# Matmuls on a buffer of zeros in the wait for the first loads

## The chip, the cores and the metric

One core of a Trainium2 chip runs the whole program. The metric is device time in microseconds (us) of one execution. Runs of the kernel before took 1066.47, 1067.73 and 1069.09 us; the median is 1067.73.

## The reference

Two groups of 512 tokens of width 1024 go through the same two layers. What matters for the change is the beginning of a layer (`c` is one conditioning row for each group):

```python
mod = jax.nn.silu(c) @ w_ada + b_ada
shift, scale, gate = jnp.split(mod, 3, axis=-1)
h = rmsnorm(x, g_norm) * (1.0 + scale[:, None, :]) + shift[:, None, :]
proj = h @ w_in
```

The projection feeds eight heads of dilated attention and four heads of retention. Their outputs are gated, joined, multiplied by `w_out`, scaled by the gate and added to `x`. A final RMS norm follows the second layer. All of it is float32.

## The kernel before

The large products are made in float32 accuracy out of rounded parts: a weight tile is split into a high half (`wH`, on ScalarE) and the rest (`wL`, on VectorE), and so is the normalised input, transposed (`hT`, 16 pieces: 8 slices k of 128 columns for each group b). `main_half` (line 839) adds three 128x512 matmuls for each k into a bank of PSUM: wH with the high half of hT, wH with its rest, wL with the high half.

**The beginning.** Lines 505 to 516 load the constants, the conditioning rows, the norm gains and the bias. VectorE clears `siluT`; ScalarE and VectorE make silu of the rows; PE transposes it and the gains (lines 523 and 524); VectorE writes them to `siluT` and `gcols`. The first columns of w_ada are then loaded in five pieces (line 760: k = 0, k = 1, then pairs). `first_mod` (578) multiplies a piece with `siluT` in column strips of 32, copies it, transposes it and makes the columns `acol` and `scol`. `first_x` (695) loads one of four tiles of x for each group, sums its squares on ScalarE, takes the inverse root on VectorE with ten tiny operations (`norm`, 685), and scales the tile on ScalarE. `first_h` (705) needs all four tiles of a group; for each k it transposes four blocks into a bank. `first_affine` (718) copies the bank to `xT` on VectorE, applies `acol` and `scol` and splits the result into hT. `prepper` (787) splits the weights. The first four items of the work list, with five output tiles, are computed early for the first group, one piece of k after another (lines 1275 to 1287); their five tiles hold five of the eight banks.

**The order.** Each engine runs its instructions in the order in which the program emits them, and that order comes from a planner in the same file. Each operation is noted with a cost (`Engine.cost`, 401), and `Plan.free["PE"]` is PE's planned time. The work is in generators; each yields a function that tells from which planned time on it is due (with a slack for what another engine makes). `pump` (214) asks all of them:

```python
now = self.free["PE"]
e = next((e for e in self.tasks if e[1]() <= now), None)
if e is None:
    t = ready()
    if t <= now:
        return
    e = min(self.tasks, key=lambda e: e[1](), default=None)
```

So what is due at PE's planned time goes first, in the order of the list, and only where nothing is due and PE would wait does the task with the earliest due time follow. The pieces' loads are issued by `pump(lambda: 0.0)` (line 1250), which runs all that is due at that time. A matmul's planned cost is `c = 0.4219 * n` for n columns, and `c + 12.0` where its operand is not float32 and its output has 128 partitions (lines 406 to 415).

All loads go through one queue, SP's. In the first 50 us it issues, in this order: constants, rows, four tiles of x, w_ada of piece 0, the first weight tile, w_ada of piece 1, four weight tiles, the rest of w_ada, and x of the second group.

Of the kernel before, what the change touches and what calls it, by code (L numbers as in the profile page):

```python
# [14 lines left out]
BF16 = mybir.dt.bfloat16  # L15
# [4 lines left out]
P = 128  # L20
# [28 lines left out]
LAT = 200.0  # L49
SLACK = {"PE": 200.0, "ACT": 400.0, "DVE": 900.0, "DMA": 1500.0}  # L50
SAME = {"DVE": 127.0}
NMAIN = 5
NBACK = 3
RLAG = 2
# [71 lines left out]
class Plan:  # L126
# [77 lines left out]
    def seen(eng, e):  # L204
        if e is None:
            return 0.0
        return e[0] + (SAME.get(eng, 0.0) if e[1] == eng else 260.0 if eng == "PE" else 180.0)

# [225 lines left out]
def trunk_kernel(  # L434
# [9 lines left out]
    V, A, T, Q = (Engine(plan, n, e) for n, e in (("DVE", nc.vector), ("ACT", nc.scalar), ("PE", nc.tensor),  # L444
                                                  ("SP", nc.sync)))
# [9 lines left out]
    H = Heap(plan, cp, "half", NHALF)  # L455
    B = Banks(plan, pp.tile([P, 8, 512], F32, name="banks"))
    W_RAW, W_W, W_T = Share(H, NRAW, NRAW, True), Share(H, NW, NW, True), Share(H, NTURN, NSURE, True)
    B_IN, B_BG = Share(B, NMAIN), Share(B, NBACK)

# [46 lines left out]
    rows, grow, th = (H.take(1, n)[:, 0:P] for n in ("rows", "grow", "th"))  # L506
# [4 lines left out]
    def mod_bias(l):  # L511
        t = H.take(1, "b6")
        Q.dma_start(t[0:6, :], b_ada[l:l + 1, :].rearrange("o (c n) -> (o c) n", n=512))
        return t

    bias = mod_bias(0)

    V.memset(siluT, 0.0)
    n16 = NB * KT
    A.activation(th[0:n16, :], rows[0:n16, :], AF.Tanh, scale=0.5)  # L520
    V.scalar_tensor_tensor(th[0:n16, :], th[0:n16, :], 1.0, rows[0:n16, :], op0=ALU.add, op1=ALU.mult)
    bk = B.take()
# [3 lines left out]
        V.tensor_scalar(siluT[:, :, b], bk[:, b * KT:(b + 1) * KT], 0.5, None, op0=ALU.mult)  # L526
    V.tensor_copy(gcols.rearrange("p l k -> p (l k)"), bk[:, 32:32 + n16])
    B.free(bk)
    H.free(rows, grow, th)

    COLS, GATES = ((0, 1), (2, 3)), ((4, 5), (4, 5))

# [736 lines left out]
    for l in range(DEPTH):  # L1269
# [77 lines left out]
        for b in range(NB):  # L1347
            for t in range(TT):
# [8 lines left out]
                for c, (n0, n1) in enumerate(LAST if final else ((0, D),)):  # L1357
                    for n, k in enumerate(KORDER):
                        pump(lambda: plan.soon(*yT[(k, b)], *wo[k]) if (k, b) in yT and k in wo else INF)
                        y, w = ([x.bitcast(F32R) for x in z] for z in (yT[(k, b)], wo[k]))  # L1360
                        for hy, hw in ((0, 0), (0, 1), (1, 0)):
                            for m in range(n0, n1, 512):
# [3 lines left out]
                                         start=(n == 0 and hy == 0 and hw == 0), stop=(n == KT - 1 and hy == 1))  # L1366
# [42 lines left out]
```

## Time and profile before

| | us |
|---|---|
| median of three runs | 1067.73 |
| the profiled execution | 1071.55 |
| span of its trace | 1069.8 |
| PE busy | 1041.6 (97%) |
| VectorE busy | 776.4 (73%) |
| ScalarE busy | 467.0 (44%) |

The profile is that of one execution. Its own time includes 1.75 us outside the span of the trace. PE is TensorE's matmuls and PEld its weight loads, DVE is VectorE, ACT is ScalarE, SP is the engine that issues the loads, and a "q" after an engine is its instruction queue. Names as `hT` or `wa` are those of the program; a buffer of the kernel's heap is reused under several names, and the trace shows only one of them (`dt` at ScalarE's first square is its scratch). Nearly every instruction carries line 385, the helper that records it, so the names tell the work apart. A float32 matmul of the small kind counts as two instructions.

### The profile page before, as it was taken

How to read it: one execution, taken by the hardware profiler on the slowest of the kernel's cores; microseconds unless marked ns; L12 is line 12 of the kernel's file. 1: busy time of each engine (PE TensorE's matmuls, PEld its weight loads, DVE VectorE, ACT ScalarE, POOL GpSimd, SP SyncE). 2: the span in 40 equal slices, each digit the busy share in tenths (PEclk: the TensorE clock that was granted, in tenths of full speed). 3: DMA queues.
4: the chain of work that ended last, by engine and by line, in shares of the span. 5: the costliest groups of instructions: out<-in, count | busy, mean ns of one | idle time of the engine just before them, and what ended most of it. 6: DMA issues, size and time to landing. Idle time of an engine off the chain costs nothing.

```text
span 1069.8 us, 14718 instructions
## 1 busy us (share of the span) xinstructions
PE 1041.6 (97%) x5443; PEld 832.8 (78%) x5443; DVE 776.4 (73%) x1616; ACT 467.0 (44%) x807; POOL 0.2 (0%) x4
## 2 busy tenths in 40 slices
PE   4999999999999999999999999999999999999997
PEld 3678676877777787777888878878888787777886
DVE  5598665688956898786547776579857896777555
ACT  6365422425533266674234562326534364665011
POOL 0000000000000000000000000000000000000000
PEclk9899999999999999999999999999999999999998
DMA  9906998048992469975222698046961749692222
GB/s 313 367 5 207 232 268 278 21 148 244 261 301 111 159 168 280 245 186 204 79 88 70 215 189 263 23 137 181 236 157 58 236 106 256 167 261 99 95 103 79
DMA packets 217336, 189.64 MB, mean 177 GB/s; under 512 B 156656, under 2 KB 167184, under 8 KB 217264
## 3 DMA queue, kind: packets, MB, share of 16 engines
q1 hardware_dynamic: 217264, 188.69, 63.0%
q8 instruction: 43, 0.70, 0.3%
q14 instruction: 29, 0.24, 0.1%
HBM read 117.34 MB, written 33.57 MB: 141 GB/s over the span
## 4 chain that ended last, share of the span: by engine, by line
PE 83%; DMA 6%; DVE 5%; SPq 3%; ACT 2%; issue 2%; DVEq 0%; ACTq 0%
PE banks L385 83%; DMA wa<-in_w_ada_dram 3%; SPq L385 3%; DMA pT<-pt 1%; DMA stk_dram<-rc 1%; DVE nst L385 1%; DMA KL<-stk_dram 1%; ACT pt L385 1%; DVE sS L385 1%; ACT sS L385 1%; DVE dt L385 1%; DVE xT L385 0%; DVE hT L385 0%; DVE rsq L385 0%; DMA stk_dram<-b 0%
## 5 line engine op out<-in xcount | busy, mean ns | idle before, releaser
L385 PE MATMUL banks<-hT,wH 128*128 128x512 f32 x1536 | 478.7, 393 | 2.9 <-DVE hT L385 2.8
L385 PEld LDWEIGHTS banks<-hT,wH 128*128 128x128 f32 x1536 | 286.9, 188 | 72.4 <-issue 9.8
L385 PE MATMUL banks<-hT,wL 128*128 128x512 f32 x768 | 300.2, 391 | 0.0
L385 PE MATMUL banks<-wo,yT 128*128 128x512 f32 (+1 forms) x792 | 176.2, 384 | 0.0
L385 PEld LDWEIGHTS banks<-hT,wL 128*128 128x128 f32 x768 | 144.7, 188 | 30.2
L385 PEld LDWEIGHTS banks<-wo,yT 128*128 128x128 f32 x792 | 145.2, 188 | 29.3 <-issue 0.4
L385 PE MATMUL banks<-wH,hT 128*128 128x256 f32 x512 | 97.5, 285 | 0.0
L385 PEld LDWEIGHTS banks<-wH,hT 128*128 128x128 f32 x512 | 81.7, 192 | 6.3 <-issue 5.4
L385 DVE TENSOR_TENSOR wL<-raw,wH 128x1024 fp32r<-128x1024 f32 x56 | 67.9, 1220 | 13.3 <-ACT wH L385 13.2
L385 PE MATMUL banks<-wL,hT 128*128 128x256 f32 x256 | 72.5, 283 | 0.0
L385 ACT ACTIVATE sS<-sS,sm 128x512 f32<-128x512 f32 x88 | 62.6, 713 | 19.0 <-DVE sm L385 18.6
L385 ACT ACTIVATE wH<-raw 128x1024 fp32r<-128x1024 f32 x56 | 58.5, 1052 | 27.5 <-DMA raw<-in_w_in_dram 21.7
L385 DVE SCALAR_TENSOR_TENSOR pt<-sS,sm,pt 128x512 f16<-128x512 f32 x88 | 61.8, 746 | 3.7 <-ACT pt L385 3.6
L385 DVE CUSTOM_DVE_ANT_0 sS<-banks,tabs 128x512 f32<-128x512 f32 x88 | 57.1, 686 | 9.3 <-PE banks L385 9.3
L385 ACT ACTIVATE pt<-sS,sm 128x512 f16<-128x512 f32 x88 | 58.7, 710 | 11.7 <-DVE sm L385 7.2
L385 ACT ACTIVATE sq<-xr 128x1024 bf16<-128x1024 f32 (+2 forms) x15 | 14.2, 944 | 92.9 <-DVE xr L385 44.3
L385 DVE TENSOR_TENSOR res<-banks,gb 128x512 f32<-128x512 f32 (+1 forms) x33 | 22.2, 671 | 43.5 <-PE banks L385 43.5
L385 PEld LDWEIGHTS banks<-wL,hT 128*128 128x128 f32 x256 | 49.0, 192 | 0.8
L385 PE MATMUL banks<-sr,rv 128*128 128x512 f32 x167 | 47.0, 392 | 0.0
L385 PE MATMUL banks<-pT,vn 128*64 128x512 f16 x384 | 45.6, 381 | 0.9 <-DMA pT<-pt 0.8
L385 PE MATMUL banks<-wa,siluT 128*32 128x128 f32 (+1 forms) x384 | 34.5, 413 | 8.7 <-DVE nst L385 5.9
L385 PEld LDWEIGHTS <-vn 128*64 128x64 f16 x384 | 21.9, 110 | 21.7 <-issue 6.4
(314 smaller groups left out, 1270.5 us busy)
## 6 DMA issues: line engine op xcount, KB each, us to landing
raw<-in_w_in_dram SPq DMA_DIRECT2D x56, 512.0 KB, 5.1
wa<-in_w_ada_dram SPq DMA_DIRECT2D x48, 512.0 KB, 7.5
KL<-stk_dram SPq DMA_DIRECT2D x49, 256.0 KB, 5.2
KS<-stk_dram SPq DMA_DIRECT2D x48, 256.0 KB, 4.7
QS<-stk_dram SPq DMA_DIRECT2D x46, 256.0 KB, 3.4
rawo<-in_w_out_dram SPq DMA_DIRECT2D x16, 512.0 KB, 4.7
stk_dram<-rs SPq DMA_DIRECT2D x31, 256.0 KB, 6.4
stk_dram<-rc SPq DMA_DIRECT2D x30, 256.0 KB, 5.9
```

The lines of the kernel that those rows point to most:

```text
L385: r = fn(*args, **kw)
```

## The change

A half buffer of zeros is taken and cleared on VectorE, ahead of `siluT`, and one bank of PSUM is taken. Matmuls of 128x128 by 128x512 in bfloat16, with zeros for both operands, write this bank, each for itself: 9 ahead of the first two transposes, 24 behind them and ahead of everything else that PE does. Bank and buffer are then given back. Nobody reads the bank's contents. The zero matmuls go through the same recording helper as all others, so their cost enters the planner.

```diff
+WARM = (9, 24)
...
+    zero = H.take(1, "zero")
+    V.memset(zero.bitcast(BF16), 0.0)
     V.memset(siluT, 0.0)
     n16 = NB * KT
+    idle = B.take()
+
+    def keep_warm(n):
+        for _ in range(n):
+            T.matmul(idle, zero.bitcast(BF16)[:, 0:P], zero.bitcast(BF16)[:, 0:512], start=True, stop=True)
+
+    keep_warm(WARM[0])
     A.activation(th[0:n16, :], rows[0:n16, :], AF.Tanh, scale=0.5)
...
     V.tensor_copy(gcols.rearrange("p l k -> p (l k)"), bk[:, 32:32 + n16])
     B.free(bk)
-    H.free(rows, grow, th)
+    keep_warm(WARM[1])
+    B.free(idle)
+    H.free(rows, grow, th, zero)
```

## Rows read from the trace of the kernel before

**Rows 1.** The profile page, parts 1 (busy time) and 4 (chain)

```profile
PE 1041.6 (97%) x5443; PEld 832.8 (78%) x5443; DVE 776.4 (73%) x1616; ACT 467.0 (44%) x807; POOL 0.2 (0%) x4
...
PE 83%; DMA 6%; DVE 5%; SPq 3%; ACT 2%; issue 2%; DVEq 0%; ACTq 0%
```

**Rows 2.** Waits of PE from 48 us: total, times, longest

```profile
PE banks L385 <- DMA wa<-in_w_ada_dram: 1.7, 4, 0.8
...
PE banks L385 <- DVE hT L385: 0.2, 1, 0.2
```

**Rows 3.** Stretches of PE: length, busy (instructions), granted clock, DMA share, GB/s

```profile
5.40:12.25 6.85, 0.95 (x6) 1.00 1.08 367
...
28.00:30.55 2.55, 0.00 (x1) 0.83 1.10 349
...
34.20:36.50 2.30, 2.30 (x41) 0.50 1.10 348
```

**Rows 4.** Groups of 12:18, 18:21.1, 24.1:25.1 us: busy us, mean ns

```profile
L385 PE MATMUL banks<-wa,siluT 128*32 128x128 f32 x32 | 4.2, 420 | 7.0 <-DVE nst L385 5.9 <-DMA wa<-in_w_ada_dram 1.1
...
L385 PE MATMUL banks<-small,x 128*128 128x128 f32 x12 | 2.8, 426 | 0.0
...
L385 PE MATMUL banks<-small,x 128*128 128x128 f32 x8 | 1.1, 281 | 0.0
```

**Rows 5.** Chain of waits up to 31 us: start, us, what

```profile
5.13 8.79 DMA wa<-in_w_ada_dram
...
13.97 3.64 PE banks L385 x30
...
18.06 6.16 PE banks L385 x49
```

**Rows 6.** Two more stretches of PE

```profile
31.14:33.70 2.56, 2.56 (x7) 0.50 1.10 348
59.72:61.76 2.04, 2.04 (x10) 1.00 0.00 0
```

**Rows 7.** Timeline of ACT and DVE, x tiles: start, us, what

```profile
0.85 0.27 DVE L385 MEMSET siluT<- 128x256 f32 x1 [0.85 <-PEq L1394]
...
6.06 0.86 DVE L385 TENSOR_SCALAR selg<-small 128x128 fp32r<-128x128 f32 x4
...
7.68 0.53 DVE L385 TENSOR_SCALAR nst<-nst 128x1 f32<-128x1 f32 x3 [0.76 <-ACT dt L385]
...
13.61 0.52 DVE L385 TENSOR_SCALAR nst<-nst 128x1 f32<-128x1 f32 x3
...
15.51 0.16 DVE L385 TENSOR_TENSOR nst<-nst 128x1 f32<-128x1 f32 x1
15.76 1.15 ACT L385 ACTIVATE x<-x,nst 128x1024 f32<-128x1024 f32 x1 [0.82 <-DVE nst L385]
```

**Rows 8.** Timeline of SP, DVE and ACT, up to hT of k = 0

```profile
10.85 1.43 SPq L385 DMA_DIRECT2D wa<-in_w_ada_dram  x1
...
18.43 0.23 DVE L385 SCALAR_TENSOR_TENSOR acol<-banks,gcols 128x1 f32<-128x1 f32 x2 [0.52 <-PE banks L385]
...
18.64 1.22 DVE L385 TENSOR_TENSOR wL<-raw,wH 128x1024 fp32r<-128x1024 f32 x1
...
24.30 1.06 ACT L385 ACTIVATE wH<-raw 128x1024 fp32r<-128x1024 f32 x1 [0.55 <-DMA raw<-in_w_in_dram]
...
26.37 0.67 DVE L385 COPY xT<-banks 128x512 f32<-128x512 f32 x1
...
29.24 0.53 DVE L385 TENSOR_SCALAR dt<-dt,acol,scol 128x512 f32<-128x512 f32 x1
29.80 0.69 DVE L385 TENSOR_TENSOR hT<-dt,hT 128x512 fp32r<-128x512 f32 x1
```

**Rows 9.** Timeline of PE, and chain of waits, 76 to 79 us

```profile
76.62 0.95 PE L385 MATMUL banks<-hT,wH 128*128 128x512 f32 x2
...
78.26 29.46 PE banks L385 x127
```

## The prediction

> **What bounds the kernel now.** I read the page first [rows 1]: PE is busy 97% of the span and carries 83% of the chain that ended last. So the time is the moment at which PE begins to work without a break, plus PE's work, plus the few waits after that. The waits after 48 us sum to 1.7 + 0.8 + 0.7 + 0.7 + 0.2 = 4.1 us [rows 2]; nearly all of PE's idle time lies ahead of 30.55 us, which is the stretch that the change touches.
>
> Second, the stretch windows of PE [rows 3]. The reader is to see that PE is idle in 5.40 to 12.25 (0.95 of 6.85 us busy) and in 28.00 to 30.55, and that from 30.55 on it is full. The granted clock reads 1.00 up to 28 us, but the durations say otherwise [rows 4]: the small matmuls on wa average 420 ns in 12 to 18 us, the transposes 426 ns in 18 to 21.1 and 281 ns after 24.1. So PE ran at 1.2 GHz until it rose to 2.4 within 21.64 to 24.2, after it had been at work since 18.06. The column does not show it; I go by durations. A second low stretch is recorded: 0.83 in the idle 28.00 to 30.55, then 0.50 until about 36.5.
>
> Third, the chain of waits up to 30.55 [rows 5]: 8.79 us of DMA for the first w_ada tiles (landed 13.92), PE's 30 matmuls of piece 0 in 3.64 us, PE again 6.16 us, then DVE alone until hT of k = 0 is split at 30.50. The change can win on the PE links of this chain, 9.8 us, and on the low clock after it.
>
> **What is added.** One memset of 128x1024 bf16: the nearest row is the 128x256 f32 memset, 0.27 us [rows 7], so 0.27 to 1.08 us by size; DVE's next work is at 5.06, so it is hidden. 33 matmuls of 512 columns: no such bf16 one is in the trace. The nearest are the main matmuls of the same shape: in 59.72 to 61.76 nine start in 2.04 us at full clock (0.227 each), in 31.14 to 33.70 six in 2.56 at half (0.427; each count in [rows 6] has one more, which only ends there). From about 1.5 us on, nine at half are 3.85 us, to 5.4: the two first transposes (5.39) move by 0 to 0.4 us, which has cover until 12.28. The 24 are 5.4 us at full clock and 10.2 at half: they end between 11.3 and 16.1. I take 12, near the full end, since PE will then have been at work without a break, as it was ahead of the rise seen in rows 4. The w_ada tile lands at 13.92, so they are hidden; if they all ran at half, piece 0 is 2.1 us late.
>
> **What moves, and this is the larger part.** The emission order of every engine comes out of the planner, and the zeros advance its clock of PE. By its cost line a 512-column bf16 matmul is 0.4219 x 512 + 12 = 228 planned ns, so the 24 put PE's planned time 5.5 planned us later at the very point where `pump(lambda: 0.0)` asks which tasks are due. (These are planner units, used for the order alone.) Before, nothing but loads is due there. After, by following the due times by hand, x tile 0 is due for its whole normalisation and tiles 1 to 3 for their squares. ACT then issues: square 0, scaled copy 0, squares 1, 2, 3, copy 1, wH of the first weights, copies 2, 3. Before, copy 0 stood behind squares 0 to 2. Square 1 now waits for DVE's chain of tile 0 and copy 0. And the four selg scalings of DVE (0.86 us), which now fill a gap at 6.06, fall behind the chain of tile 0.
>
> In trace time [rows 7]: square 0 ends 7.65, DVE's chain 0 runs 7.68 to 9.75, copy 0 1.15 us to 10.93, square 1 with its read to 12.2, then DVE's chains 1 to 3 at 1.97 us each to 18.2. Before, chain 3 ended at 15.67. So DVE is 2.5 us late with x, and all transposes of x (they need all four tiles) wait until copy 3 ends at 19.35, against 18.32 before. Piece 0 now leaves PE about 15.8 instead of 17.6, but DVE takes it up only at 18.2. What the faster PE wins there, the x chain gives back.
>
> After that, by hand again, PE has piece 1 ahead of the transposes of x, and DVE has: copy of piece 0, wL, acol/scol, copy of piece 1, wL, acol/scol, xT, wL, xT, wL, scaling of xT, wL, split of hT. Piece 1's second tile was issued at 10.85; with the first one's 8.79 us it lands about 19.65 (no later than 21.64, where PE did not wait for it). Its 32 matmuls take 3.6 us at half (30 took 3.62) and 1.8 at full clock as half of that. DVE's copy of it ends 21.85 at full clock, 23.65 at half. Behind it stand 4 wL x 1.22 + 0.23 for acol + 2 x 0.67 + 0.53 + 0.69 = 7.67 us of DVE [rows 8], so hT of k = 0 is complete at 29.5 or 31.3, against 30.49: **-1.0 or +0.8**. I take -1.0, as PE is then in a nearly unbroken run and the floor by the last early weight (ACT 24.30 + 1.06, wL 1.22, 0.53, 0.69: 27.8) does not bind.
>
> One price more: only 3 banks stay spare beside the 5 early ones, and each holds a group of 4 transposes until DVE copies it. With DVE late, 5 of the 8 groups are done before the main matmuls and 12 transposes fall into the full stretch, where nothing hides them. Eight took 1.1 us at full clock, twelve 2.8 at half [rows 4]: **+1.65** (to +2.8; 0 if I misplace them).
>
> By the Trainium skill ("TensorE: Matmul & The Clock Gate", Part 4, on PE-mode transposes) the full clock does not engage for transposes, and the twelve would be priced at 2.8. The trace disagrees: 281 ns after 24.1 against 426 before.
>
> The second low stretch (30.55 to 36.5, 5.95 us, half lost: 3.0 us) I leave as it is: PE still idles before the split of hT, from about 26.4 to 29.6, and a shorter idle stretch ended in the fall before. Bounds: -3.0 to 0.
>
> From 48.31 to 78.26 the chain runs over ACT and DVE (x of the second group, decays, hT) [rows 9], and PE waits at its end 0.22 us, with 0.33 more inside the pair at 76.62 (0.95, against 0.62 for the pair before it). If PE comes later this takes **-0.55** back; if it comes earlier, DVE's chain keeps most of that gain unless its start moves too.
>
> **Sum**: -1.0 + 1.65 - 0.55 = +0.1 us. The profiled execution took 1071.55 (span 1069.8 and 1.75 around it), so 1071.65; the median of the runs shown, 1067.73, is 3.82 lower, so **1067.8**. What can be told from no change is 0.3%, 3.2 us; this is no change.
>
> **Rivals.**
> *PE stays fast.* The clock, once up, stays up through the first waits, the x chain costs less than I work out, and the second fall is gone too: hT at the floor, 27.8, is -2.7, the low stretch -3.0, together 1062.0. For it: PE's links on the chain are 9.8 us. Against it: the clock fell in the idle stretch of 2.55 us from 28.00 on [rows 3], and idle stretches of about 2 us (12 to 13.9) and 2.7 (15.8 to 18.5) remain.
> *The order falls luckily.* All later choices of the planner see a shifted PE time; at best the 4.1 us of later waits go: about 1063.8. Nothing but the 4.1 bounds it.
> *Warmth is lost in the gap* (the slower side). PE has nothing between 15.8 and 18.5, the clock falls there, piece 1 runs at half: hT +0.8, twelve transposes at half +2.8, and -0.55: +3.05, 1070.8; from a fall ahead of about 20 us on it decides. For it: the same fall.
> [...]
> *Zeros do not raise the clock.* The 24 end at 16.1, piece 0 at 19.7, piece 1 about 24.0, hT 31.95 (+1.5), +2.8, -0.55: +3.75, 1071.5.
>
> **Chances.** My forecast 0.42; PE stays fast 0.18; lucky order 0.14; warmth lost 0.18 (half of it over the 0.3%, as later waits add to it); zeros useless 0.08. The order of work after 60 us may shift either way by as much as the 4.1 us of waits. So faster 0.32, same 0.44, slower 0.24. Range for 8 in 10: from below the lucky cases, 1061, to above the useless zeros, 1072.5. The forecast's own range is 1065.5 to 1070.
>
> **What would show it.** ACT's order: copy 0 directly behind square 0, copy 3 after 18 us. Right: DVE's x chain ends near 18. Wrong: the old order, with copy 3 at 15.8. wa matmuls of pieces 0 and 1 far below 420 ns (420 for piece 1 would be the slower rival). The second main matmul at 29.6 (below 28.5: PE stays fast; above 31: slower). Twelve transposes of x after it. The granted clock at 0.50 again for 4 to 6 us behind it. PE's waits after 48 us near 4 us; a sum over 8 would make the prediction wrong from a place that I could not price.

## The result, and the profile after

| | before | after |
|---|---|---|
| median of four runs each, us | 1068.03 (1066.47 to 1069.09) | 1080.7 (1080.14 to 1082.15) |
| ratio, with its 95% interval | | 1.0105 (1.0083 to 1.0127) |
| the profiled execution, us | 1071.55 | 1082.15 |
| span of its trace, us | 1069.8 | 1080.3 |

The change makes the kernel 1.05% slower by the ratio, which is 11.2 us; the medians of the table lie 12.67 us apart. The forecast was no change, 1067.8, and the range ended at 1072.5. The cause of the main slower rival, lost warmth, did not decide the time. One execution of a later run (LAT 150 with zeros) took 5379.28 us and is left out of its ratio.

The page after, parts 1 (busy time) and 4 (chain), the answers to [rows 1]:

```profile
PE 1049.5 (97%) x5476; PEld 833.6 (77%) x5476; DVE 776.1 (72%) x1617; ACT 468.5 (43%) x808; POOL 0.2 (0%) x4
...
PE 83%; DMA 6%; DVE 4%; SPq 3%; ACT 1%; issue 1%; ACTq 0%; DVEq 0%
```

PE has 33 instructions and 7.9 us more of busy time, and its share of the chain is as before. The page alone does not say where 10.5 us of span came from: the 33 zero matmuls stand in a wait, and do not lengthen the span by their own time. The profiled execution of before is itself 3.5 us above its median, so these 10.5 us tell two executions apart and not the medians. I cut the trace at 48 us, where the beginning is over. These are the windows of PE (stretch, length, busy and count, granted clock, DMA share, GB/s), first of the kernel before, then after:

```profile
0.00:48.00 48.00, 32.06 (x356) 0.93 1.02 338
48.00:1069.80 1021.80, 1009.58 (x5088) 1.00 0.62 170
```

```profile
0.00:48.00 48.00, 38.55 (x397) 0.93 1.01 336
48.00:1080.30 1032.30, 1010.93 (x5081) 1.00 0.61 168
```

From 48 us on PE is busy 1.35 us longer (1010.93 against 1009.58) and idle 21.37 us instead of 12.22: **9.15 of the 10.5 us are new idle time behind the stretch that the change touches.** The waits of PE from 48 us on name it (total, times, longest), against the five rows and 4.1 us of [rows 2] (first a row of before that does not stand there):

```profile
PE banks L385 <- DMA pT<-pt: 0.8, 2, 0.5
```

```profile
PE banks L386 <- DMA wa<-in_w_ada_dram: 4.8, 4, 2.6
PE banks L386 <- DMA pT<-pt: 3.3, 4, 1.6
PE banks L386 <- DVE yT L386: 2.9, 2, 2.0
PE banks L386 <- DMA QS<-stk_dram: 1.1, 1, 1.1
PE banks L386 <- DMA KL<-stk_dram: 0.7, 2, 0.6
PE banks L386 <- ACT yT L386: 0.4, 1, 0.4
```

The six of the kernel after sum to 13.2 us. Three of them were not there before (yT twice, QS); those on w_ada and pT have grown by 3.1 and 2.5; before's waits on yr and hT are gone. The largest single wait, 2.6 us, ends at 122.78. SP's queue shows what it waits for (start, us, what), and PE's timeline the end of it:

```profile
103.79 14.34 SPq L386 DMA_TRANSPOSE pT<-pt  x4
118.22 1.01 SPq L386 DMA_DIRECT2D wa<-in_w_ada_dram  x2
...
122.78 2.92 PE L386 MATMUL banks<-wa,siluT 128*32 128x512 f32 x8 [2.55 <-DMA wa<-in_w_ada_dram]
```

PE's row for the next eight of this shape in the kernel before:

```profile
128.82 1.07 PE L385 MATMUL banks<-wa,siluT 128*32 128x512 f32 x8
```

Two tiles of w_ada are issued at 118.22, behind four transposes by DMA that hold SP's queue for 14.34 us, and PE's order has the eight matmuls on them at 120.2. Before, the pair of loads behind four transposes was issued 4.5 us later, at 122.75 (its row stands below), and the next eight matmuls of this shape began at 128.82, without a wait: PE now asks for them at 120.23, 8.6 us earlier, while SP sends them only 4.5 us earlier. This wait has a second price, in the windows of PE around it and of the beginning:

```profile
14.65:18.00 3.35, 3.31 (x30) 0.55 1.21 305
...
29.02:32.10 3.08, 3.08 (x7) 0.51 1.10 349
...
120.20:122.80 2.60, 0.05 (x3) 1.00 0.88 306
122.80:126.40 3.60, 3.45 (x10) 0.70 1.07 256
126.40:132.00 5.60, 5.60 (x24) 0.89 1.16 265
```

After the wait the granted clock is 0.70 for 3.60 us and 0.89 for 5.60: 0.30 x 3.60 + 0.11 x 5.60 = 1.7 us lost. That is more than the 1.35 us by which PE is busier from 48 us on, so by this count PE has 0.35 us less work left at 48 us than it had before: all that the zeros win in the beginning of this execution.

### The profile page after: what moved, and what is told of

Its sections match the earlier page's. It is cut to its first block, busy times and chain, and to the rows that moved or that the text cites. A ratio compares the mean times of both kernels' runs of the same rounds, so it can differ in the third digit from the quotient of the medians.

```text
span 1080.3 us, 14817 instructions
## 1 busy us (share of the span) xinstructions
PE 1049.5 (97%) x5476; PEld 833.6 (77%) x5476; DVE 776.1 (72%) x1617; ACT 468.5 (43%) x808; POOL 0.2 (0%) x4
## 4 chain that ended last, share of the span: by engine, by line
PE 83%; DMA 6%; DVE 4%; SPq 3%; ACT 1%; issue 1%; ACTq 0%; DVEq 0%
PE banks L386 83%; SPq L386 3%; DMA wa<-in_w_ada_dram 2%; DMA pT<-pt 1%; DMA KL<-stk_dram 1%; DVE hT L386 1%; DMA raw<-in_w_in_dram 1%; DVE pt L386 1%; DVE wL L386 1%; DMA KS<-stk_dram 1%; DVE sS L386 0%; DVE rc L386 0%; ACT pt L386 0%; DMA stk_dram<-rc 0%; DVE rsq L386 0%
## 5 line engine op out<-in xcount | busy, mean ns | idle before, releaser
L386 PEld LDWEIGHTS banks<-hT,wH 128*128 128x128 f32 x1536 | 287.0, 189 | 74.3 <-issue 13.2
L386 ACT ACTIVATE sS<-sS,sm 128x512 f32<-128x512 f32 x85 | 60.4, 712 | 21.1 <-DVE sm L386 20.6
L386 ACT ACTIVATE sq<-xr 128x1024 bf16<-128x1024 f32 (+2 forms) x18 | 17.3, 963 | 115.2 <-DVE xr L386 71.3
```

What stands on the lines that cost most here:

```text
L386: r = fn(*args, **kw)
```

## The experiments

Each ratio is against runs of the kernel before on the same chip. Two theories stood at first. **O**: the zeros cost nothing where they stand, but as they go through the planner they advance its time of PE, the whole order is drawn anew, and this draw is worse. **A**: the added work itself costs (PE's sequence, the clock, the bank, the buffer). The expectations call it rival Z; what they call A is the bank and the buffer alone.

**The zeros without the planner.** They are issued past the recording helper, so the planned order is that of before, instruction by instruction; in the traces, PE, DVE and ACT keep it, apart from the zeros and one memset.

```diff
+    zero = diff.bitcast(BF16)[:, 0:512]
+    nc.vector.memset(zero, 0.0)
...
+            nc.tensor.matmul(B.t[:, 7, :], zero[:, 0:P], zero, start=True, stop=True)
```

> The 33 zero matmuls stand where the change has them, but are issued without a note in the planner, out of a buffer and a bank that it does not count, so that every other instruction has the order of the kernel before. Theory O (the loss is the order that the planner draws once its PE clock is moved): no loss; PE runs piece 0 and the first transposes at full clock, hT of k = 0 is complete about 29.1 us instead of 30.49, and the time is 1064 to 1067 against 1068.0. Rival Z (the zero matmuls themselves cost PE or its clock later on): 1078 or more, as with the change.

**The planner without the zeros.** Each zero matmul is noted with its cost, none is issued.

```diff
-            T.matmul(idle, zero.bitcast(BF16)[:, 0:P], zero.bitcast(BF16)[:, 0:512], start=True, stop=True)
+            z = zero.bitcast(BF16)
+            plan.note("PE", T.cost("matmul", [idle], [z[:, 0:P], z[:, 0:512]]), [idle], [z[:, 0:P], z[:, 0:512]])
```

> The planner notes the 33 zero matmuls, with buffer and bank, but none of them is issued: the order of every engine is that of the change, without zeros on the chip (the zero buffer is still cleared). Theory O: as slow as the change, 1080 to 1084, since the low clock of the beginning comes back. Rival Z: 1066 to 1070, as the kernel before.

Measured: zeros alone 1073.08 against 1069.25, ratio **1.0024** (1.0005 to 1.0043); order alone 1077.71, ratio **1.0086** (1.0057 to 1.0116). Neither time lies in the range that O had given it, but by ratio both are nearer to O than to Z. What the planner makes of the zeros, with not one zero matmul issued, carries 0.86 of the 1.05%; that is the new order together with the buffer and the bank that the noted zeros take, which this run does not part. In the traces the order of PE (without the zeros), DVE, ACT and SP agrees with the kernel after, instruction by instruction. Part of the loss is low clock: the five executions have a mean granted clock of 0.9916, the 30 of before beside them 0.9969. That is an estimated 5.7 us of the 8.7 by which their mean times differ. Its two largest waits of PE from 48 us on are again of the kinds that the kernel after shows:

```profile
PE banks L386 <- DMA pT<-pt: 3.1, 2, 2.1
PE banks L386 <- DVE yT L386: 1.6, 2, 0.9
```

But the longest wait of the kernel after is missing. The loads behind the four transposes, and the eight matmuls on them:

```profile
116.62 1.13 SPq L386 DMA_DIRECT2D wa<-in_w_ada_dram  x2
...
121.37 1.81 PE L386 MATMUL banks<-wa,siluT 128*32 128x512 f32 x8
```

The transposes held SP's queue for 12.45 us here and for 14.34 with the zeros, in the same order. So the wait of 2.55 us is not the order's alone; this run loses its time elsewhere, most visibly at 472 to 490 us, where PE waits on yT four times and the granted clock reads 0.81.

The run of the zeros alone is the more instructive one, for it has the change as it was meant and still gains nothing. Its timeline of PE:

```profile
14.25 1.93 PE L386 MATMUL banks<-wa,siluT 128*32 128x128 f32 x30 [1.28 <-DMA wa<-in_w_ada_dram]
...
28.95 0.50 PE L386 MATMUL banks<-hT,wH 128*128 128x512 f32 x1 [1.37 <-DVE hT L386]
...
75.21 0.50 PE L386 MATMUL banks<-hT,wH 128*128 128x512 f32 x1 [0.22 <-DVE hT L386]
...
114.04 1.05 PE L386 MATMUL banks<-wa,siluT 128*32 128x512 f32 x4 [1.48 <-DMA wa<-in_w_ada_dram]
```

Piece 0 takes 1.93 us where it took 3.64 [rows 5], the second main matmul starts at 28.95 where it started at 30.55, and no later fall of the clock is recorded. At 75.21 it starts the very matmul that started at 78.26 before [rows 9]: 3.05 us ahead. Not all of this belongs to the zeros. The profiled execution of before had its clock fall from 28 us on [rows 3], and many have not: of 107 executions of before in these runs 52 have a mean granted clock of 0.998 or more, which leaves under 3 us of lost clock in the whole span, and the profiled one has 3.4 in its first 48 us (0.07 x 48). A run without zeros that has the same order of PE (w_ada on a second queue, below) starts this matmul at 76.15, 2.1 us ahead.

Then a new wait of 1.48 us on w_ada stands at 114.04. The two tiles were issued at 106.19 (107.59 before), and the second is there at 115.33 (115.60 before): issued 1.4 us earlier, it lands 0.3 us earlier, and that is all that is left of PE's lead. SP's queue behind them, before and then with the zeros alone:

```profile
108.52 14.18 SPq L385 DMA_TRANSPOSE pT<-pt  x4
122.75 1.24 SPq L385 DMA_DIRECT2D wa<-in_w_ada_dram  x2
```

```profile
107.20 16.39 SPq L386 DMA_TRANSPOSE pT<-pt  x4
123.64 1.05 SPq L386 DMA_DIRECT2D wa<-in_w_ada_dram  x2
```

The same four transposes are issued 1.3 us earlier, hold the queue 2.2 us longer, and the loads behind them go out 0.9 us later. In this execution starting earlier did not mean finishing earlier. It is no rule: the eight matmuls that begin at 128.82 before begin as follows with the zeros alone, with more zeros in the second gap, and in the change with PE's time put back (the last two are below):

```profile
128.55 1.81 PE L386 MATMUL banks<-wa,siluT 128*32 128x512 f32 x8
```

```profile
126.00 1.75 PE L386 MATMUL banks<-wa,siluT 128*32 128x512 f32 x8
```

```profile
125.19 1.90 PE L386 MATMUL banks<-wa,siluT 128*32 128x512 f32 x8
```

The lead is 0.3, 2.8 and 3.6 us. The second loses it at 178.40, in a wait of 2.75 us on w_ada; the third, the fastest of ten executions, keeps it as long as its order is that of before (the same matmul at 895.23 and 891.33). The first ends 2.5 us behind before, and loses most of that after 130 us. So the traces do not agree on where the lead goes.

**More warmth.** If the clock is the point, the next gap of PE (from 26.4 to hT) should be worth filling too. 20 more zero matmuls of 256 columns follow the first main matmul, again unseen by the planner.

```diff
+            if fill:
+                for _ in range(fill.pop()):
+                    nc.tensor.matmul(out[:, 0:256], zero2[:, 0:P], zero2, start=False, stop=False)
```

> As the run with unseen zeros, and 20 more unseen zero matmuls of 256 columns behind the first main matmul, added into its bank, where PE waits 2.56 us for the split of hT. Theory O with the low clock as a cost of its own: the clock does not fall near 30 us, the main matmuls from there on take 0.227 us each and not 0.427, and 1 to 3 us are won on top of the first run: 1061 to 1066. Rival Z: slower than the first run.

Measured: 1072.22, ratio 1.0019 (0.9999 to 1.0038), no better than without them. It was to reach 1061 to 1066. The trace of the zeros alone was already free of the second fall, so there was nothing for it to win there.

**Other draws of the order.** If the order is what counts, other numbers of planned zeros must give other times, whether zeros run or not. First the change with 34 for 24, then the change with PE's planned time put back behind the 24, then 8, 20 and 15 planned ones of which none is issued.

```diff
-WARM = (9, 24)
+WARM = (9, 34)
```

> The change with 34 zeros in the second group instead of 24; the planner sees them and draws a third order. The ten more end before the first w_ada tile lands (14.6 us), so on the chip they cost nothing. Theory O: the time is that of another draw and differs from the change's 1080.7 by more than 3 us, to either side (the planner's own end is 5 planned us earlier than for the change). Rival Z: 1080 to 1083.

```diff
+    now = plan.free["PE"]
     keep_warm(WARM[1])
+    plan.free["PE"] = now
```

> The change as it is, 33 zeros through the planner with buffer and bank, but PE's planned time is put back behind the 24 to what it was ahead of them. The planner then draws the order of the kernel before (its planned times agree up to PE's matmul 4414 of 5211). Theory O, by the planned clock: 1.000 to 1.005 of the kernel before, as with unseen zeros (1.0024). Rival A (the buffer half and the bank that the zeros take shift all later buffers): 1.008 or more, as with the change.

```diff
-WARM = (9, 24)
+WARM = (9, 8)
```

> Only the planner sees zeros, none is issued, and 8 in the second group instead of 24: enough that the square of x's first tile is due early, too few for the rest. Theory O: another draw, with a time of its own between 0.998 and 1.012 of the kernel before, not the 1.0086 of the 24. If a moved planned clock were bad by itself, the loss would go with its size: 1.003.

> Only the planner sees zeros, 20 in the second group. Its own end is 1.3 planned us ahead of the kernel before, where that of the 24 is 2.5 behind. Theory O with a planner that knows its work: 0.997 to 1.001 of the kernel before. If the planner does not know what a draw costs on the chip (as for the 34, which it put 2.3 ahead and the chip at 1.0026): anywhere from 0.998 to 1.012. If the loss goes with the size of the shift: 1.007.

> Only the planner sees zeros, 15 in the second group. The planner itself puts the end 18.8 planned us behind that of the kernel before, the worst of the draws. Theory O with a planner that knows its work: 1.015 to 1.02. If the planner does not know: anywhere from 0.998 to 1.012. If the loss goes with the size of the shift: 1.0055.

Then the kernel before without any zeros, with another constant of the planner, `LAT`, the planned time (200) from the end of an instruction to the engine that takes its result. It changes nothing on the chip except the order.

```diff
-LAT = 200.0
+LAT = 190.0
```

> The kernel before without any zeros, with the planner's latency constant 190 instead of 200: a new draw of the order that has nothing to do with the change; the planner puts its end 0.1 planned us behind that of the kernel before. Theory L (the order of the kernel before is a lucky draw, and nearly any other loses, whatever makes it): 1.002 to 1.010. Rival N (draws scatter about the planner's end, and the loss belongs to the orders that the zeros draw): 0.997 to 1.002.

> As above with 205 instead of 200; the planner puts the end 0.9 planned us ahead. Theory L: 1.002 to 1.010. Rival N: 0.996 to 1.001.

Measured, in the order of the planner's own end (its planned time at the end of the program, as difference to before, in its us):

| kernel | planned end | ratio (95%) |
|---|---|---|
| 15 planned, none issued | +18.8 | 1.0191 (1.0145 to 1.0236) |
| 24 planned, none issued | +2.5 | 1.0086 (1.0057 to 1.0116) |
| the change (24) | +2.5 | 1.0105 (1.0083 to 1.0127) |
| the change, PE's time put back | +0.4 | 1.0059 (1.0038 to 1.0080) |
| LAT 190, no zeros | +0.1 | 1.0019 (1.0002 to 1.0035) |
| 8 planned, none issued | 0.0 | 1.0062 (1.0040 to 1.0083) |
| LAT 205, no zeros | -0.9 | 1.0029 (1.0012 to 1.0046) |
| 20 planned, none issued | -1.3 | 1.0057 (1.0038 to 1.0076) |
| the change with 34 | -2.3 | 1.0026 (1.0005 to 1.0046) |

All nine are slower than before, by 0.2 to 1.9%, whether zeros run or not. A planned latency of 190 instead of 200 is enough for 0.19%, at the edge between the ranges of L and N; 205, with 0.29%, lies in that of L. That the loss goes with the number of planned zeros fails at 8 (0.62%, not 0.3) and at 15 (1.91% in two executions, not 0.55). The planner's end sorts them roughly, with exceptions (0.0 gave 0.62%, +0.1 gave 0.19%). What stands out is before itself: at its planned end it beats every neighbour, down to a planned gain of 2.3. The run with PE's time put back was to fall at 1.005 or below by O and at 1.008 or above by A; at 1.0059 it decided nothing. Its order is that of before for PE's first 4,400 matmuls. What the rest of the order, or the buffer and the bank that the zeros take, add to the 0.24% of unseen zeros stays open.

**Is it SP's queue?** The loads of w_ada behind the first pieces go through GpSimd's queue, so that no transpose stands ahead of them; once with the order of before and no zeros, once with zeros unseen by the planner.

```diff
+    L = Engine(plan, "SP", nc.gpsimd)
...
-            Q.dma_start(t, split(w_ada[l, k * P:(k + 1) * P, c * D:(c + 1) * D], 2))
+            L.dma_start(t, split(w_ada[l, k * P:(k + 1) * P, c * D:(c + 1) * D], 2))
```

> The kernel before with the later loads of w_ada (32 of 512 KB) issued from GpSimd's queue instead of SP's, where they stand behind the DMA transposes of the attention; planner and order as before. If SP's queue sets the pace from 107 to 180 us: PE's waits for wa (1.7 us) go, 0.997 to 0.999. If the transfers themselves do (DMA share 1.1 in 110 to 140 us): 0.999 to 1.003, other tiles coming later instead.

> The same with the 33 unseen zeros. PE was 3.0 us ahead at 77 us in the run with unseen zeros and had lost it by 127 us, while SP's queue was 3 us ahead at 106 and level at 134. If SP's queue sets the pace there, the 3 us are kept and the waits for wa (3.5 us) go: 0.993 to 0.998. If the transfers set it: 1.000 to 1.004, no better than the unseen zeros alone (1.0024).

Measured: 1089.51, ratio 1.0179 (1.0153 to 1.0205), and 1084.87, ratio 1.0152 (1.0111 to 1.0192). Both are far off what either theory expected. In the first, PE's wait for w_ada is gone, and the transposes wait instead. The DMA issues in 100 to 200 us (what, count, median us from issue to landing) of before, then of the run with the second queue and no zeros, and at last PE's waits from 48 us on in that run:

```profile
pT<-pt SPq DMA_TRANSPOSE x8, 5.9
```

```profile
pT<-pt SPq DMA_TRANSPOSE x8, 19.3
```

```profile
PE banks L385 <- DMA vn<-vt: 9.6, 1, 9.6
PE banks L385 <- DMA pT<-pt: 7.1, 2, 6.4
```

With eight transposes landing in 19.3 us instead of 5.9, PE waits 16.7 us for what they deliver, and its granted clock reads 0.91 over 100 to 200 us, where it read 1.00 before. So taking w_ada out of SP's queue does not help this stretch: a load that is let past the transposes delays them by more than it gains. That the transfers themselves set the pace fits this and is not shown, for the second queue is also of another kind (the profile lists it as software_dynamic, SP's as hardware_dynamic), which was not tried by itself.

**Does a good order win, and do zeros then help?** By then it was open whether before is simply a draw that few others reach. Three kernels have an order whose planned end is well ahead of before's: LAT 150 without zeros, the same order with the 33 zeros unseen, and the change with 8 zeros and LAT 140. The first was picked as the best of several hundred planned orders.

> The kernel before, no zeros, latency constant 150: the planner puts its end 5.4 planned us ahead of that of the kernel before, the best of several hundred draws looked at. Over the draws measured so far the chip's loss follows the planner's end roughly 1:1, with the kernel before 5 to 6 us better than that line. By the line: 0.999 to 1.002. If the kernel before is a lucky draw and the planner's end says little near it: 1.002 to 1.008. If the planner's end holds against the kernel before too: 0.993 to 0.997.

> The same order with the 33 unseen zeros. If the start that they win is given back where the transfers set the pace (94 to 180 us): within 0.002 of e13. If it was given back only because the order of the kernel before happens to leave no room: 0.001 to 0.004 below e13.

> The change with 9 and 8 zeros that the planner sees, and latency constant 140: the planner puts the end 5.1 planned us ahead of the kernel before. By the line: 0.999 to 1.003. If draws with seen zeros are bad by themselves: 1.005 or more.

| kernel | planned end | us | ratio (95%) |
|---|---|---|---|
| LAT 150, no zeros | -5.4 | 1067.44 | 0.9979 (0.9962 to 0.9995) |
| LAT 150, 33 zeros unseen | -5.4 | 1070.19 | 1.0007 (0.9995 to 1.0019) |
| the change with 8, LAT 140 | -5.1 | 1066.76 | 0.9968 (0.9952 to 0.9983) |

The orders planned five ahead beat both kernels, by 0.2% without zeros, between two of its expected ranges, and by 0.3% in the change with 8, where 0.1% was the most expected (how much of that is its order and how much its zeros was not separated).

The zeros in an unchanged order cost again: 1070.19 against 1067.44, 0.26%, after 0.24% in the first pair. Neither expectation had that. In the traces of this second pair they win little: the second main matmul starts at 25.91 instead of 26.41, and at 39 us PE is 0.2 us behind and stays so up to 107 us. Then comes the place where it loses. PE's timeline with the zeros, and a window of PE behind that wait:

```profile
122.87 3.31 PE L386 MATMUL banks<-wa,siluT 128*32 128x512 f32 x8 [2.84 <-DMA wa<-in_w_ada_dram]
```

```profile
122.50:126.00 3.50, 3.13 (x8) 0.54 1.16 266
```

The timeline without them:

```profile
119.59 1.05 PE L385 MATMUL banks<-wa,siluT 128*32 128x512 f32 x4 [1.08 <-DMA wa<-in_w_ada_dram]
```

The same matmuls wait 1.08 us without zeros and 2.84 with them, and the longer wait is followed by a clock of 0.54 (0.46 x 3.50 = 1.6 us lost), the pattern of the kernel after. SP's queue ahead of these loads, without and then with the zeros:

```profile
102.25 12.66 SPq L385 DMA_TRANSPOSE pT<-pt  x4
```

```profile
103.54 14.88 SPq L386 DMA_TRANSPOSE pT<-pt  x4
```

The transposes begin 1.3 us later and hold the queue 2.2 us longer, so the tiles are sent 3.5 us later, at 118.47 instead of 114.96. Why the transposes take longer in the same order is not settled.

## Why the prediction was wrong, point by point

The kernel after by its own trace. PE in the beginning:

```profile
1.45 3.73 PE L386 MATMUL banks<-zero 128*128 128x512 bf16 x9 [1.45 <-DVE zero L386]
...
5.76 5.35 PE L386 MATMUL banks<-zero 128*128 128x512 bf16 x24
...
14.65 3.32 PE L386 MATMUL banks<-wa,siluT 128*32 128x128 f32 x30 [1.28 <-DMA wa<-in_w_ada_dram]
...
19.54 1.93 PE L386 MATMUL banks<-wa,siluT 128*32 128x128 f32 x30 [0.19 <-DMA wa<-in_w_ada_dram]
...
29.02 0.79 PE L386 MATMUL banks<-hT,wH 128*128 128x512 f32 x1 [2.44 <-DVE hT L386]
...
36.22 0.60 PE L386 MATMUL banks<-small,x 128*128 128x128 f32 x4
...
42.68 0.66 PE L386 MATMUL banks<-small,x 128*128 128x128 f32 x4
```

ACT and DVE in the same stretch, to be set beside [rows 7, 8]:

```profile
9.70 1.15 ACT L386 ACTIVATE x<-x,nst 128x1024 f32<-128x1024 f32 x1 [2.19 <-DVE nst L386]
10.76 1.04 ACT L386 ACTIVATE th<-x 128x1024 bf16<-128x1024 f32 x1
...
16.93 2.25 ACT L386 ACTIVATE x<-x,nst 128x1024 f32<-128x1024 f32 x2
...
17.78 0.16 DVE L386 TENSOR_TENSOR nst<-nst 128x1 f32<-128x1 f32 x1
18.00 0.28 DVE L386 COPY th<-banks 64x128 f32<-64x128 f32 x1
...
28.29 0.68 DVE L386 TENSOR_TENSOR hT<-th,hT 128x512 fp32r<-128x512 f32 x1
```

1. **What bounds the kernel**: right. PE's share of the chain did not change, and the time came out of its waits.
2. **What is added**: right, and hidden. Nine zeros took 3.73 us (3.85 expected), the 24 end at 11.1 (12 expected, 11.3 the early bound).
3. **Warmth**: half right. The clock fell behind the waits for the two tiles of piece 0 (1.00 up to 14.65, 0.55 in 14.65 to 18.00), so piece 0 left PE at 18.0 and not at 15.8. It cost nothing, since DVE took it up at 18.00 (18.2 expected). Piece 1 ran at full clock, 1.93 us. The slower rival, warmth lost, had the fall in the gap behind piece 0; the fall came ahead of it, and it did not decide the time.
4. **What moves in the beginning**: right to a few tenths. Copy 0 (9.70) stands behind square 0 and ahead of square 1 (10.76), DVE's chain of x ends at 17.94 (18.2), copy 3 at 19.18 (19.35), hT of k = 0 is complete at 28.97 (29.5): -1.5 where I had -1.0. Exactly twelve transposes of x fall into the full stretch (four each at 36.22, 37.35 and 42.68), the +1.65.
5. **The second low stretch**: mis-sized within its bounds. It lasted 3.08 us and not 5.95, which is 1.4 us won that I had left at nothing. It belongs to the execution as much as to the kernel: by their mean clock, 52 of the 107 executions of before cannot have had it in full.
6. **The wait at 78.26**: gone, as priced; no wait on hT is left after 48 us.
7. **The step that failed**: "The order of work after 60 us may shift either way by as much as the 4.1 us of waits." The waits of before bound what a new order can *remove*; they do not bound what it can *add*. The waits went from 4.1 to 13.2, and the longest brought a low clock of 1.7 us with it. The same order without the zeros cost 0.86%, 8.5 us by the medians and twice that bound. I had made a rival of the lucky order, with 0.14, and none of the unlucky one, the same mechanism with the other sign, though the prediction itself names a sum over 8 as what it could not price.

The sum with measured terms: the beginning gives 0.35 us of work by the windows. By my terms it should be 1.5 + 1.4 - 1.65 = 1.25; the 0.9 between them is not resolved (against the run of the order alone PE is 1.2 us ahead, the same matmul at 118.03 and 119.24). Then +9.15 of idle time and +1.7 of clock: -0.35 + 9.15 + 1.7 = 10.5, the difference of the spans. The sum has to close, since the 0.35 was found from it.

What is shown and what is not. Shown: what the planner makes of the zeros (the order, with the buffer and the bank) makes 0.86 of the 1.05% without a single zero matmul; and in two pairs with equal order the zeros make the kernel no faster, but 0.24 and 0.26% slower. Their faster beginning is 1.6 us at the second main matmul in the first pair; in the second it is 0.5 us, and gone at 39 us. Not shown: the last 0.19% of the change (the intervals overlap; the 0.24% of the zeros would cover it), what buffer and bank do apart from the order, and the mechanism by which the zeros cost 0.2 to 0.3%. Mending the places of the new order one by one was not tried.

## What to carry to other kernels

Where a planner writes the order, every instruction that it sees is also an input to it: try a filler unseen by the planner and planned without being issued, and only then judge the filler. The waits of a tuned order bound what a new order can win, not what it can lose, so a redrawn order deserves a rival on the slower side that is priced well above those waits, unless the planner puts it well ahead (here five of its us won 0.2 to 0.3%, two did not). And time won in the beginning is not yet won at the end: of three traces with the zeros, PE's order of before and one queue, one lost the lead by 129 us, one by 180, and one kept it. Where executions differ by as much as the effect, one pair of traces does not tell where the time went.

## What the runs showed of the hardware

- One wait of 2.6 us on PE in the middle of full work was followed by a granted clock of 0.70 and 0.89 over 9.2 us: it cost 2.6 + 1.7 us. A wait of 2.84 in another run was followed by 0.54 over 3.5 us. Waits of 0.39, 0.94 and 1.96 us between 480 and 487 us of the kernel after were followed by 1.00.
- The same program does not always see its clock fall: 107 executions of the kernel before had mean granted clocks of 0.993 to 0.999. The 52 at 0.998 or more took 1068.3 us on average, the 12 at 0.994 or less 1072.7.
- Transfers moved to a second queue can lengthen the others more than they gain: transposes by DMA went from 5.9 to 19.3 us with w_ada on GpSimd's queue, and the kernel lost 1.8%.
- The granted clock reads 1.00 in 12 to 18 us of before while durations show half speed [rows 4]; in the kernel after, where PE had been at work before, it reads 0.55 for the same matmuls at 391 ns. Durations are the safer witness at the start of a trace.
